# A hybrid GDN/HGRN2 block on one Trainium2 core: gates and HGRN values projected token-major, four heads at a time

## The chip, the cores and the metric

The kernel runs on one core of one Trainium2 chip. The metric is the device time of one execution in microseconds (us), as the median over runs. The engines are named as in the profile: PE (TensorE, matrix products into PSUM), DVE (VectorE), ACT (ScalarE), POOL (GpSimd) and SP (SyncE, which here only issues DMAs). Each engine works through its own instructions in order; semaphores hold an instruction until what it needs is done.

## The reference

One layer for 256 tokens (T) of width 2048 (D), all in float32:

```
n = rms_norm(h, norm_mix_w)
proj = n @ w_in                      # GDN: q, k, v, z and a, b;  HGRN2: q, f, i, g
# GDN, 8 heads of 128
qkv = silu(causal_conv4(qkv));  q, k l2-normalized
o = gated_delta_rule_chunked(q, k, v, beta, g)       # chunks of 64, a unit-lower system per chunk
y_a = head_rms_norm(o, norm_w) * silu(z)
# HGRN2, 8 heads of 128
forget = lb + (1 - lb) * sigmoid(f);  key = (1 - lb) * sigmoid(-f)
o = hgrn2_chunked(silu(q), key, i, log(forget))
y_b = head_rms_norm(o, norm_w) * silu(g)
h = h + concat(y_a, y_b) @ w_out
h = h + relu(rms_norm(h, norm_ffn_w) @ w1)**2 @ w2
out = rms_norm(h, norm_final_w)
```

In head_rms_norm the mean of squares runs over the 128 columns of a head, one value for each token and head.

## The kernel before

**Weights.** Every weight matrix streams through as tiles of 128 x 2048 (1 MB), 208 in all: 64 for the input projection (w_in), 16 for w_out, 64 each for the two feed-forward products (FF1, FF2). SP loads them in order into three buffers (`wpool`). To keep float32 accuracy, `split` (L111) cuts each half of a tile (1024 columns) into `hi`, rounded by ACT to fp32r (L117), and `lo`, the rest, by DVE (L118); the pairs lie in three buffers (`spool`). The activations are split once in the same way (`xT`, `hT`, `yTa`, `yTb`: first T columns hi, next T lo). PE computes hi·hi, hi·lo and lo·hi.

**Input projection.** `project` (L265) is feature-major: it takes two tiles and forms two 128-feature outputs over all 256 tokens. The weight is the stationary operand; one product of 512 columns (L281: both parts of `xT`) and one of 256 (L282) form a pair, 16 pairs for each tile. Two accumulators from `psA` (four PSUM banks of 512 columns in all) hold the result. L288 to L290 sum the two halves (ACT and DVE) and scale by `rB`, the norm's reciprocal for each token as a row repeated on every partition (DVE for HGRN, POOL for GDN). A head calls `project` twice: GDN for q, k and then v, z; HGRN for q, f and then i, g.

**Mixer.** Eight GDN heads (`gdn_mix`), each: convolution (L320, L322), silu, the gate SZ from z (L329), transposed v, normalized q and k, the key products `pk` and `pk`'s second half (L363, L364), whose decayed results (L367) are stored to DRAM (`scr_a`, L373). After the eighth, `gdn_invert` (L406) inverts all 32 x 32 diagonal blocks on POOL in 31 steps between L413 and the DMA of L424, and loads them back as `Xn` (L427). Eight HGRN heads follow (`hgrn_mix`): sigmoids, gate SZ (L531), scan (L542), ten operations on 256 columns for the decays of five levels (L548 and L563, five each), small products into `pd` and `pa` (L578 to L593), masks (L596, L600), the matrix `A`, and the head's output `poh`, 128 features by 256 tokens (L612, L613). `gdn_solve` (L430) finishes the triangular solve from the first HGRN head on (`SOLVE_AT` 9) and forms the GDN outputs two heads at a time. `finish_heads` squares the output, sums over features with a product by a matrix of ones (`pm`, L393 and L394, also hi and lo), takes the reciprocal root over all tokens and features (L395, L396), multiplies by it and by SZ (L397, L398) and splits the result into `yTa` (heads 0 to 11) or `yTb` (12 to 15).

**Order.** The body names heads in sequence, each head's projection one ahead of its mix; a tile framework with a scheduler then interleaves the instructions of each engine, and the order is fixed when the program is built. Buffers that are declared once (`bufs=1`) make a later writer wait for the last reader.

**Rest.** w_out runs as two halves of the output columns, eight tiles each, over the 16 heads' `yT`; the last product of the first half needs head 15's `yTb`. FF1 and FF2 follow. `h` (2 MB, the residual) is loaded by SP before the last two w_in tiles, into the memory that holds PA (key matrices of the first five heads).

Of the kernel before, what the change touches and what calls it, by code (L numbers as in the profile page):

```python
# [73 lines left out]
def hybrid_block(ctx: ExitStack, tc: tile.TileContext, x, xt, w_in, w_ab, params, w_out, w_ff1, w_ff2,  # L74
# [80 lines left out]
    sums = mp.tile([P, 4, T], F32, tag="u", name="sums")  # L155
# [109 lines left out]
    def project(base, hd, chunk, dsts):  # L265
        accs = [acc_a() for _ in range(2)]
        for kh in range(2):
            first = base == 0 and hd == 0 and chunk == 0
            if first:
                w = w_first[kh]  # L270
            else:
                w = wtile()
                SP.dma_start(w, w_in[((base > 0) * NH + hd) * 4 + chunk * 2 + kh])
# [12 lines left out]
        for g in range(2):  # L286
            lot = mp.tile([P, T], F32, tag="lot", name="lot", bufs=2)
            ACT.copy(lot, accs[g][:, T:])  # L288
            DVE.tensor_tensor(out=lot, in0=accs[g][:, 0:T], in1=lot, op=ALU.add)
            (POOL if base == 0 else DVE).tensor_tensor(out=dsts[g], in0=lot, in1=rB, op=ALU.mult)  # L290
# [15 lines left out]
    def gdn_project(hd):  # L306
        pre = mp.tile([P, 4, T], F32, tag="gx", name="pre").rearrange("p a t -> p (a t)")[:, 0:3 * (T + 3)]
        pre = pre.rearrange("p (a t) -> p a t", a=3)
        R = mp.tile([P, 4, T], F32, tag="R", name="R", bufs=RB)
        POOL.memset(pre[:, :, 0:3], 0.0)  # L310
# [4 lines left out]
    def gdn_mix(hd, pre, R):
        for i in range(3):
# [9 lines left out]
        DVE.scalar_tensor_tensor(out=u, in0=R, scalar=0.0, in1=u, op0=ALU.min, op1=ALU.subtract)
# [20 lines left out]
        DVE.tensor_tensor(out=qk, in0=qk, in1=u[:, 2:4, :], op=ALU.mult)  # L347
# [33 lines left out]
    def finish_heads(h0, nh, po, sz, scale, bank):  # L381

        n = nh * T
# [5 lines left out]
        shi = mp.tile([P, n], F32R, tag="Xn" if nh == 2 else "sh", name="shi")  # L389
        slo = mp.tile([P, n], F32R, tag="Yd" if nh == 2 else "vv", name="slo")  # L390
        ACT.copy(shi, sq)
        DVE.tensor_tensor(out=slo, in0=sq, in1=shi.bitcast(F32), op=ALU.subtract)
        PE.matmul(pm, lhsT=ones_r, rhs=shi, start=True, stop=False)  # L393
        PE.matmul(pm, lhsT=ones_r, rhs=slo, start=False, stop=True)  # L394
        ACT.activation(sq, pm, AF.Ln, bias=eps, scale=scale / P)  # L395
# [3 lines left out]
        src, hs = (yTa, h0) if h0 < NYA else (yTb[0], h0 - NYA)  # L399
        yv = sq.rearrange("p (a t) -> p a t", a=nh)  # L400
        hi, lo = src[:, hs:hs + nh, 0:T], src[:, hs:hs + nh, T:]
        split(yv, None, hi, lo)
# [27 lines left out]
    def gdn_solve(Xn):  # L430
# [67 lines left out]
        for pair in range(NH // 2):  # L498
            po = sv("po")
            for n in range(2):  # L500
                hd, c = 2 * pair + n, n * T
                PE.matmul(po[:, c:c + T], lhsT=V[:, hd, 0, :], rhs=PA(hd)[:, 0, 0:T], start=True, stop=False)
                PE.matmul(po[:, c + P:c + T], lhsT=V[:, hd, 1, :], rhs=PA(hd)[:, 0, T:384], start=False, stop=True)
            finish_heads(2 * pair, 2, po, SZ[:, 2 * pair:2 * pair + 2, :].rearrange("p a t -> p (a t)"), 1.0 / P, sv)


    def hgrn_project(hd):
        R = mp.tile([P, 4, T], F32, tag="R", name="R", bufs=RB)
        project(4112, hd, 0, (R[:, 0, :], R[:, 1, :]))
        project(4112, hd, 1, (R[:, 3, :], R[:, 2, :]))  # L510
        return R

    def hgrn_mix(hd, R):

        pv = mx("pvh")
        for hf in range(2):
            PE.transpose(pv[:, hf * P:(hf + 1) * P], R[:, 3, hf * P:(hf + 1) * P], ident)
        vv = mp.tile([P, 2, P], F32, tag="vv", name="vv")
        ACT.copy(vv.rearrange("p a e -> p (a e)"), pv[:, 0:T])
        u = mp.tile([P, 4, T], F32, tag="u", name="u", bufs=UB)  # L520
        sigmoid_parts(u[:, 0:3, :], R[:, 0:3, :], 3 * T)
        DVE.scalar_tensor_tensor(out=u[:, 3, :], in0=R[:, 1, :], scalar=0.0, in1=u[:, 1, :], op0=ALU.max, op1=ALU.add)
        DVE.scalar_tensor_tensor(out=u[:, 0:3, :], in0=R[:, 0:3, :], scalar=0.0, in1=u[:, 0:3, :],
                                 op0=ALU.min, op1=ALU.subtract)
# [6 lines left out]
        DVE.scalar_tensor_tensor(out=SZ[:, (NH + hd) % NRING, :], in0=R[:, 2, :], scalar=gnw[:, 1:2], in1=u[:, 2, :],  # L531
                                 op0=ALU.mult, op1=ALU.mult)
# [294 lines left out]
```

## Time and profile before

| what | before |
|---|---|
| median of 3 runs | 1277.36 us (1276.52 to 1277.49) |
| the profiled execution | 1277.5 us, span 1275.6 us |
| mean granted PE clock in it | 0.99 |
| last head's `poh` (L612), start | 496.38 us |
| FF1, first product (L704) | 555.44 us |
| weights and others moved | 229.65 MB, mean 180 GB/s |

The span runs from the first to the last instruction that the trace shows. Times in quoted rows count from its start. A timeline row holds: start, duration, engine, line, operation, output<-inputs, shapes, count, and in brackets how long the engine stood idle before it and what ended that. A group row holds: line, engine, operation, names, shapes, count | busy us, mean ns of one | idle us before them and what ended most of it. A windows row holds for one stretch the busy time of each engine with its number of instructions, then the granted PE clock (1.00 is full), the share of DMA time and GB/s.

### The profile page before, as it was taken

How to read it: one execution, taken by the hardware profiler on the slowest of the kernel's cores; microseconds unless marked ns; L12 is line 12 of the kernel's file. 1: busy time of each engine (PE TensorE's matmuls, PEld its weight loads, DVE VectorE, ACT ScalarE, POOL GpSimd, SP SyncE). 2: the span in 40 equal slices, each digit the busy share in tenths (PEclk: the TensorE clock that was granted, in tenths of full speed). 3: DMA queues.
4: the chain of work that ended last, by engine and by line, in shares of the span. 5: the costliest groups of instructions: out<-in, count | busy, mean ns of one | idle time of the engine just before them, and what ended most of it. 6: DMA issues, size and time to landing. Idle time of an engine off the chain costs nothing.

```text
span 1275.6 us, 18490 instructions
## 1 busy us (share of the span) xinstructions
PE 1243.4 (97%) x7290; PEld 1054.2 (83%) x7290; DVE 857.5 (67%) x1200; ACT 674.2 (53%) x972; POOL 178.7 (14%) x224
## 2 busy tenths in 40 slices
PE   6999999998999999999999999999999999999997
PEld 5888888877788887888888888888888888888885
DVE  8789999889978996566555565555555555555556
ACT  7567677655667774555444444444444444444453
POOL 4233433278310130000000000000000000000000
PEclk9999999998999998999999999999999999999999
DMA  7445555543424544455555555555555555555552
GB/s 290 167 154 192 172 177 190 182 141 131 151 101 169 196 165 165 160 203 198 177 187 197 173 191 191 176 195 185 178 198 199 197 195 189 188 191 195 198 203 95
DMA packets 34646, 229.65 MB, mean 180 GB/s; under 512 B 4408, under 2 KB 5184, under 8 KB 7808
## 3 DMA queue, kind: packets, MB, share of 16 engines
q1 hardware_dynamic: 32256, 225.32, 50.1%
q0 software_dynamic: 1728, 2.11, 1.3%
q8 instruction: 57, 0.93, 0.3%
q10 hardware_dynamic: 576, 1.05, 0.2%
q14 instruction: 29, 0.24, 0.1%
HBM read 225.83 MB, written 2.63 MB: 179 GB/s over the span
## 4 chain that ended last, share of the span: by engine, by line
PE 91%; DVE 3%; POOL 3%; issue 2%; DMA 1%; ACT 0%; SPq 0%; POOLq 0%; DVEq 0%; ACTq 0%
PE acc L281 15%; PE acc L721 14%; PE accb L721 13%; PE accb L704 9%; PE acc L704 9%; PE acc L282 8%; PE acc L659 7%; PE accb L705 5%; PE acc L705 5%; POOL Xt L419 1%; POOL X L421 1%; DVE xT L163 1%; DMA big<-in_xt_dram 1%; PE pk L363 1%; DVE E L548 0%
## 5 line engine op out<-in xcount | busy, mean ns | idle before, releaser
L118 DVE TENSOR_TENSOR lo<-w,hi 128x1024 fp32r<-128x1024 f32 x408 | 511.9, 1256 | 362.9 <-ACT hi L117 362.3
L117 ACT CAST hi<-w 128x1024 fp32r<-128x1024 f32 (+1 forms) x416 | 432.7, 1042 | 442.4 <-PE accb L721 177.0
L281 PE MATMUL acc<-xT,hi 128*128 128x512 f32 x1024 | 363.7, 401 | 10.0 <-ACT hi L117 8.3
L282 PE MATMUL acc<-xT,lo 128*128 128x256 f32 x1024 | 283.6, 286 | 4.5 <-DVE lo L118 4.3
L281 PEld LDWEIGHTS acc<-xT,hi 128*128 128x128 f32 x1024 | 192.1, 191 | 50.1 <-ACT hi L117 8.3
L282 PEld LDWEIGHTS acc<-xT,lo 128*128 128x128 f32 x1024 | 195.7, 192 | 11.6 <-DVE lo L118 5.8
L704 PE MATMUL acc<-hT,hi 128*128 128x512 f32 x512 | 181.3, 399 | 0.0
L704 PE MATMUL accb<-hT,hi 128*128 128x512 f32 x512 | 180.8, 398 | 0.0
L721 PE MATMUL accb<-hi,gs 128*128 128x512 f32 x496 | 170.5, 389 | 0.0
L705 PE MATMUL accb<-hT,lo 128*128 128x256 f32 x512 | 143.2, 281 | 0.0
L705 PE MATMUL acc<-hT,lo 128*128 128x256 f32 x512 | 142.8, 281 | 0.0
L721 PE MATMUL acc<-hi,gs 128*128 128x512 f32 x496 | 133.4, 389 | 0.0
L704 PEld LDWEIGHTS accb<-hT,hi 128*128 128x128 f32 x512 | 96.1, 188 | 23.8
L704 PEld LDWEIGHTS acc<-hT,hi 128*128 128x128 f32 x512 | 96.1, 188 | 23.3
L159 POOL TENSOR_TENSOR fin<-fin,cst 128x1 f32<-128x1 f32 x2 | 1.1, 566 | 776.9 <-PE accb L721 769.5
L721 PEld LDWEIGHTS accb<-hi,gs 128*128 128x128 f32 x496 | 93.1, 188 | 19.4
L721 PEld LDWEIGHTS acc<-hi,gs 128*128 128x128 f32 x496 | 93.1, 188 | 19.2
L705 PEld LDWEIGHTS acc<-hT,lo 128*128 128x128 f32 x512 | 96.5, 189 | 0.2
L705 PEld LDWEIGHTS accb<-hT,lo 128*128 128x128 f32 x512 | 96.5, 189 | 0.1
L721 PE MATMUL accb<-lo,gs 128*128 128x512 f32 x248 | 95.8, 389 | 0.0
L721 PE MATMUL acc<-lo,gs 128*128 128x512 f32 x248 | 77.2, 389 | 0.0
L721 PEld LDWEIGHTS accb<-lo,gs 128*128 128x128 f32 x248 | 46.6, 188 | 9.7
(248 smaller groups left out, 1275.2 us busy)
## 6 DMA issues: line engine op xcount, KB each, us to landing
w<-in_w_ff_dram SPq DMA_DIRECT2D x128, 1024.0 KB, 4.9
w<-in_w_in_dram SPq DMA_DIRECT2D x62, 1024.0 KB, 5.0
w<-in_w_out_dram SPq DMA_DIRECT2D x16, 1024.0 KB, 4.9
big<-in_xt_dram SPq DMA_DIRECT2D x4, 512.0 KB, 7.7
w<-in_w_in_dram SPq DMA_DIRECT2D x4, 512.0 KB, 7.9
h<-in_x_dram SPq DMA_DIRECT2D x2, 1024.0 KB, 9.0
dt<-scr_g POOLq DMA_DIRECT2D x8, 128.0 KB, 5.6
nfw<-in_norm_final_w_dram SPq DMA_DIRECT2D x1, 1024.0 KB, 4.4
```

The source lines that it names most:

```text
L117: ACT.copy(hi, w)
L118: eng.tensor_tensor(out=lo, in0=w, in1=hi.bitcast(F32), op=ALU.subtract)
L163: DVE.scalar_tensor_tensor(out=dst[:, k, T:2 * T], in0=pt, scalar=wcol, in1=dst[:, k, 0:T].bitcast(F32), op0=ALU.mult, op1=ALU.subtract)
L281: PE.matmul(accs[g], lhsT=hi[:, kk, g, :], rhs=xT[:, k, :], start=(k == 0), stop=False)
L282: PE.matmul(accs[g][:, T:], lhsT=lo[:, kk, g, :], rhs=xT[:, k, 0:T], start=False, stop=(k == KT - 1))
L363: PE.matmul(pk0, lhsT=R[:, 1, 0:P], rhs=qk.rearrange("p a t -> p (a t)"), start=True, stop=True)
L419: POOL.tensor_tensor(out=t3, in0=X[:, j, j + 1:].unsqueeze(2).to_broadcast([np_, nr, ncol]), in1=X[:, j, 0:ncol].unsqueeze(1).to_broadcast ...
L421: POOL.tensor_tensor(out=X[:, j + 1:, 0:ncol], in0=X[:, j + 1:, 0:ncol], in1=t3, op=ALU.subtract)
L659: PE.matmul(accs[2 * hf + c], lhsT=st, rhs=ww[:, c * 512:(c + 1) * 512], start=(k == 0 and a == 0 and ww is hi), stop=(k == 2 * NH - 1 and ...
L704: PE.matmul(accs[f], lhsT=hi[:, cs], rhs=hT[:, k, :], start=(k == 0), stop=False)
L705: PE.matmul(accs[f][:, T:], lhsT=lo[:, cs], rhs=hT[:, k, 0:T], start=False, stop=(k == KT - 1))
L721: PE.matmul(accs[hf][c], lhsT=gs[:, a + hf * P:a + hf * P + P], rhs=ww[:, cs], start=(f == 0 and a == 0 and ww is hi), stop=(f == NF - 1 a ...
```

## The change

What was feature-major for each head becomes token-major for four heads at once, for three of the eight outputs: the HGRN values i, the HGRN gates g and the GDN gates z.

- `project_tokens` takes four tiles and forms 512 features (four heads) for both token halves: `xT` is now the stationary operand and the weight the moving one, 24 products of 512 columns for each tile (L318). The two accumulators are copied out by ACT alone, with the norm's factor as a per-partition scale (`rcol`, L322). Results go to single tiles `vi`, `szg`, `szz`, which the second group of four heads reuses. 24 of the 64 tiles go this way.
- `gates_tokens` applies silu to such a group once, on 1024 columns (L325 onwards); the gates SZ of each head, with the norm weight in them, are gone.
- `project` now serves q and k (or q and f) of a head, and v of two GDN heads. The sigmoid work of a GDN head has 768 columns in place of 1024, that of an HGRN head 512 in place of 768.
- Mixer outputs are token-major: `po` and `poh` have tokens on the partitions, so i needs no transpose.
- `finish_heads` squares on ACT with a row sum for each head and token half (L439), takes the reciprocal root of those sums only (L440, L441), and scales each 128 x 128 block by it and by the gate in one DVE operation (L445). PE then transposes the result (`pt`, L452), and ACT and DVE split it with the norm weight as scale (L458, L459).
- The order of heads in the body is new. After the inversion: g's first group, q/f of head 1, mix 0, z's first group, q/f 2, solve, finish of GDN heads 0 to 3, mix 1, z's second group, q/f 3, finish of GDN heads 4 to 7, mix 2, q/f 4, mix 3, i's second group, g's second group, and then q/f and mixes of heads 4 to 7. (i's first group and q/f 0 are projected during the last GDN head.)

The core of the diff:

```
-        project(0, hd, 0, (pre[:, 0, 3:], pre[:, 1, 3:]))
-        project(0, hd, 1, (pre[:, 2, 3:], R[:, 3, :]))
...
+    def project_tokens(tag, name):
+        accs = [acc_a() for _ in range(2)]
+        for kq in range(4):
+            w, _ = w_next()
+            for q in range(2):
+                hi, lo = split(w[:, q * 1024:(q + 1) * 1024], 1024)
+                for kk in range(2):
...
+                    for hf in range(2):
+                        for a, ww in ((0, hi), (T, hi), (0, lo)):
+                            PE.matmul(accs[hf], lhsT=xT[:, k, a + hf * P:a + hf * P + P], rhs=ww[:, cs],
+                                      start=(k == 0 and a == 0 and ww is hi), stop=(k == KT - 1 and ww is lo))
+        dst = mp.tile([P, 2, 512], F32, tag=tag, name=name)
+        for hf in range(2):
+            ACT.activation(dst[:, hf, :], accs[hf], AF.Copy, scale=rcol[:, hf:hf + 1])
+        return dst
+
+    def gates_tokens(tag, name):
+        Z = project_tokens(tag, name)
+        u = mp.tile([P, 2, 512], F32, tag="gx", name="uz", bufs=2)
+        sigmoid_parts(u, Z, 1024)
+        DVE.scalar_tensor_tensor(out=u, in0=Z, scalar=0.0, in1=u, op0=ALU.min, op1=ALU.subtract)
+        ACT.activation(u, u, AF.Exp)
+        DVE.tensor_tensor(out=Z, in0=Z, in1=u, op=ALU.mult)
+        return Z
...
-        sq = mp.tile([P, n], F32, tag=f"fsq{nh}", name="fsq", bufs=1)
-        ACT.activation(sq, po, AF.Square)
-        pm = bank("pm")[:, 0:n]
...
-        ACT.activation(sq, pm, AF.Ln, bias=eps, scale=scale / P)
-        ACT.activation(sq, sq, AF.Exp, scale=-0.5)
-        DVE.tensor_tensor(out=sq, in0=po, in1=sq, op=ALU.mult)
-        DVE.tensor_tensor(out=sq, in0=sq, in1=sz, op=ALU.mult)
...
-        split(yv, None, hi, lo)
+        for hf in range(2):
+            for n in range(nh):
+                ACT.activation(sq, po[hf][:, n * P:(n + 1) * P], AF.Square, accum_out=ss[:, hf, n:n + 1])
+        ACT.activation(ss, ss, AF.Ln, bias=eps, scale=scale / P)
+        ACT.activation(ss, ss, AF.Exp, scale=-0.5)
...
+                DVE.scalar_tensor_tensor(out=y[:, hf, s], in0=po[hf][:, s], scalar=ss[:, hf, n:n + 1], in1=sz[:, hf, s],
+                                         op0=ALU.mult, op1=ALU.mult)
...
+            pt = bank("pt")[:, 0:w * T]
...
+                    PE.transpose(pt[:, n * T + hf * P:n * T + hf * P + P], y[:, hf, (m * w + n) * P:(m * w + n + 1) * P],
+                                 ident)
...
+            ACT.activation(hi, pt, AF.Copy, scale=gnw[:, group:group + 1])
+            DVE.scalar_tensor_tensor(out=lo, in0=pt, scalar=gnw[:, group:group + 1], in1=hi.bitcast(F32), op0=ALU.mult,
+                                     op1=ALU.subtract)
...
+    hgrn_mix(0, qf[0], vi, sz)
+    szz = gates_tokens("szz", "szz")
+    qf.append(hgrn_qf())
+    gdn_solve(Xn)
+    gdn_finish(0, szz)
+    hgrn_mix(1, qf[1], vi, sz)
+    szz = gates_tokens("szz", "szz")
+    qf.append(hgrn_qf())
+    gdn_finish(1, szz)
+    hgrn_mix(2, qf[2], vi, sz)
+    qf.append(hgrn_qf())
+    hgrn_mix(3, qf[3], vi, sz)
+    vi = project_tokens("vi", "vi")
+    sz = gates_tokens("szg", "szg")
+    for n in range(4, NH):
+        if n + 1 < NH:
+            qf.append(hgrn_qf())
+        hgrn_mix(n, qf[n], vi, sz)
```

The order that the scheduler makes of this is shown at three places. The first is PE around head 3's output. Before, `poh` of that head stands between projection products (L281, L282 are the pair of `project`; `pw_3088` belongs to the solve):

```order
L281 MATMUL acc<-xT,hi 128x512
L282 MATMUL acc<-xT,lo 128x256
L281 MATMUL acc<-xT,hi 128x512
L485 MATMUL pw_3088<-V,Y 128x128 x4
L282 MATMUL acc<-xT,lo 128x256
L281 MATMUL acc<-xT,hi 128x512
L612 MATMUL poh<-A,vv 128x256
L613 MATMUL poh<-A,vv 128x128
L282 MATMUL acc<-xT,lo 128x256
```

Now, on PE at the same place, from head 2's transposes on (L295 and L296 are the pair of `project`, here for head 5's q and f; L318 would be a token-major projection):

```order
L452 MATMUL pt<-cst,szg 128x128 x2
L631 MATMUL pd<-E 32x32 x32
L634 MATMUL pd<-gx 32x64 x8
L640 MATMUL pa<-E 32x32 x4
L644 MATMUL pa<-E 64x64 x2
L646 MATMUL pa<-L 128x128
L665 MATMUL poh<-vi,A 128x128
L666 MATMUL poh<-vi,A 128x128
L667 MATMUL poh<-vi,A 128x128
L295 MATMUL acc<-xT,hi 128x512
L296 MATMUL acc<-xT,lo 128x256
```

The projection products that stood among a head's small products have moved: none stands between head 2's transposes and head 3's output, and the next projection comes behind both.

The second place is ACT at the same heads (`A` is a head's matrix, L439 reads its output, L322 copies a token-major group out of its accumulators), as it is now:

```order
L663 COPY A<-pa 32x2x32 x2
L439 ACTIVATE fsq,ss<-poh 128x128
L322 ACTIVATE vi<-acc,rcol 128x512 x2
L439 ACTIVATE fsq,ss<-poh 128x128
L440 ACTIVATE ss<-ss,cst 128x2
L441 ACTIVATE ss<-ss 128x2
L458 ACTIVATE yTa<-pt,gnw 128x256
L322 ACTIVATE szg<-acc,rcol 128x512 x2
L117 CAST hi<-w 128x1024
```

The copies of i's second group (`vi`) stand behind the first reading of head 3's output, and those of g's second group (`szg`) behind that head's finish. Before, no such copy exists: two of L288 follow each projection.

The third place is SP's list of loads:

```order
-L273 DMA w<-in_w_in_dram 128x2048 x60
-L642 DMA h<-in_x_dram 128x2048 x2
-L273 DMA w<-in_w_in_dram 128x2048 x2
...
+L280 DMA w<-in_w_in_dram 128x2048 x56
+L715 DMA h<-in_x_dram 128x2048 x2
+L280 DMA w<-in_w_in_dram 128x2048 x6
```

The residual's two loads stand ahead of the last six w_in tiles now, in place of the last two. POOL's list loses the HGRN operations of heads that now come after the inversion in the order; its 31 steps are the same.

More of the change, by code (lines that the diff above doesn't have):

```diff
@@ L154, in hybrid_block @@
     junk = mp.tile([P, 1024], F32, tag="big", name="junk")
-    sums = mp.tile([P, 4, T], F32, tag="u", name="sums")
+    sums = mp.tile([P, 4, T], F32, tag="gx", name="sums", bufs=2)
+    rcol = cpool.tile([P, 2], F32, tag="rcol", name="rcol")
     def rstd(dst, src):
@@ L176, in row_scales @@
             PE.matmul(prb[:, 0:T], lhsT=ones, rhs=sums[:, c, :], start=(c == 0), stop=(c == 3))
+        for hf in range(2):
+            for c in range(4):
+                PE.matmul(prb[:, T + hf:T + hf + 1], lhsT=sums[:, c, hf * P:(hf + 1) * P], rhs=ones[:, 0:1],
+                          start=(c == 0), stop=(c == 3))
         ACT.activation(rB, prb[:, 0:T], AF.Ln, bias=eps, scale=1.0 / D)
         ACT.activation(rB, rB, AF.Exp, scale=-0.5)
+        ACT.activation(rcol, prb[:, T:T + 2], AF.Ln, bias=eps, scale=1.0 / D)
+        ACT.activation(rcol, rcol, AF.Exp, scale=-0.5)
     par = cpool.tile([P, 6, NH], F32, tag="par", name="par")
@@ L262, in gates, with w_next, project @@
         POOL.dma_start(scr_g, gr)
-    def project(base, hd, chunk, dsts):
+    tiles = [0]
+    def w_next():
+        n = tiles[0]
+        tiles[0] += 1
+        if n < 2:
+            return w_first[n], True
+        w = wtile()
+        SP.dma_start(w, w_in[n])
+        return w, False
+    def project(dsts, eng=POOL):
         accs = [acc_a() for _ in range(2)]
         for kh in range(2):
[L268 to L273, printed above, removed]
+            w, first = w_next()
             for q in range(2):
@@ L304, in hybrid_block, with pre, gdn_qk, gdn_v @@
     scr_x = dpool.tile([NH, 2, 4, 32, 32], F32, tag="scr_x", name="scr_x")
[L306 to L310, printed above, removed]
-        project(0, hd, 0, (pre[:, 0, 3:], pre[:, 1, 3:]))
-        project(0, hd, 1, (pre[:, 2, 3:], R[:, 3, :]))
-        return pre, R
-    def gdn_mix(hd, pre, R):
+    pres = {}
+    def pre(hd):
+        if hd not in pres:
+            p = mp.tile([P, 4, T], F32, tag="gx", name="pre", bufs=2).rearrange("p a t -> p (a t)")[:, 0:3 * (T + 3)]
+            pres[hd] = p.rearrange("p (a t) -> p a t", a=3)
+            POOL.memset(pres[hd][:, :, 0:3], 0.0)
+        return pres[hd]
+    def gdn_qk(hd):
+        p = pre(hd)
+        project((p[:, 0, 3:], p[:, 1, 3:]))
+    def gdn_v(pair):
+        project([pre(2 * pair + n)[:, 2, 3:] for n in range(2)])
+    def gdn_mix(hd):
+        pre = pres[hd]
+        R = mp.tile([P, 3, T], F32, tag="R", name="R", bufs=RB)
         for i in range(3):
@@ L379, in yT, with finish_heads @@
         return yTa[:, k, a:b] if k < NYA else yTb[0][:, k - NYA, a:b]
[L381 to L383 removed]
+    def finish_heads(h0, nh, po, sz, group, scale, bank):
         if h0 >= NYA and not yTb:
             yTb[0] = ypool.tile([P, 2 * NH - NYA, 2 * T], F32R, tag="yb", name="yTb")
[L386 to L402 removed]
@@ L497, in gdn_solve @@
             ACT.copy(V[:, hs, 1, :], pw.rearrange("p (a e) -> p a e", a=4))
[L498 to L504, printed above, removed]
@@ L507, in hgrn_project, with gdn_finish @@
[L507 to L510, printed above, removed]
-        return R
[L513 to L523, printed above, removed]
+    def gdn_finish(quad, sz):
+        po = [sv("po") for _ in range(2)]
+        for n in range(4):
+            hd, s = 4 * quad + n, slice(n * P, (n + 1) * P)
+            PE.matmul(po[0][:, s], lhsT=PA(hd)[:, 0, 0:P], rhs=V[:, hd, 0, :], start=True, stop=True)
+            PE.matmul(po[1][:, s], lhsT=PA(hd)[:, 0, P:T], rhs=V[:, hd, 0, :], start=True, stop=False)
+            PE.matmul(po[1][:, s], lhsT=PA(hd)[:, 0, T:384], rhs=V[:, hd, 1, :], start=False, stop=True)
+        finish_heads(4 * quad, 4, po, sz, 0, 1.0 / P, mx)
@@ L531, in hgrn_mix @@
[L531 to L532 removed]
+        DVE.tensor_scalar(KQ[:, 0, :], u[:, 2, :], oml[:, hd:hd + 1], None, ALU.mult)
         lf = view(u, 0, [[2 * T, 2], [1, T]])
```

100 lines of the change are left out of this document (66 added, 34 removed).

## The prediction

> **What bounds the kernel now.** I read the page first (busy shares, then the chain that ended last), then windows of the stretch that the change rewrites, then TensorE's idle rows in it.
>
> ```profile
> PE 1243.4 (97%) x7290; PEld 1054.2 (83%) x7290; DVE 857.5 (67%) x1200; ACT 674.2 (53%) x972; POOL 178.7 (14%) x224
> ...
> PE 91%; DVE 3%; POOL 3%; issue 2%; DMA 1%; ACT 0%; SPq 0%; POOLq 0%; DVEq 0%; ACTq 0%
> PE acc L281 15%; PE acc L721 14%; PE accb L721 13%; PE accb L704 9%; PE acc L704 9%; PE acc L282 8%; PE acc L659 7%; PE accb L705 5%; PE acc L705 5%; POOL Xt L419 1%; POOL X L421 1%; DVE xT L163 1%; DMA big<-in_xt_dram 1%; PE pk L363 1%; DVE E L548 0%
> ```
>
> Over the whole program TensorE (PE) is the bound: 1243.4 of a span of 1275.6 us. The stages differ, though. The windows give start:end, length, then busy time of PE, weight loads, VectorE (DVE), ScalarE (ACT), GpSimd (POOL), and the granted clock:
>
> ```profile
> core 0: us, PE busy (x) PEld busy (x) DVE busy (x) ACT busy (x) POOL busy (x), PEclk, DMA share, GB/s
> 33.00:247.00 214.00, 214.00 (x1200) 182.20 (x1199) 188.01 (x264) 145.72 (x206) 71.17 (x82) 1.00 0.54 177
> 247.00:335.00 88.00, 78.21 (x611) 66.20 (x613) 76.91 (x121) 48.30 (x82) 65.55 (x91) 0.92 0.41 141
> 335.00:504.00 169.00, 166.06 (x1576) 142.37 (x1561) 142.94 (x258) 115.38 (x200) 25.45 (x32) 1.00 0.45 158
> 504.00:556.00 52.00, 51.73 (x225) 42.47 (x226) 27.07 (x32) 23.21 (x31) 0.00 (x0) 0.94 0.47 164
> ```
>
> In the GDN stage (33 to 247) PE never stops, but DVE is already at 188.01 of 214. In 247 to 335 (the inversion on POOL beside the first HGRN heads) PE loses 9.79 us and runs at 0.92. These are its idle rows, with the last wait of the mixer at 504:
>
> ```profile
> 289.13 0.58 PE L282 MATMUL acc<-xT,lo 128*128 128x256 f32 x1 [2.81 <-DVE lo L118]
> ...
> 297.99 0.33 PE L578 MATMUL pd<-E 128*32 128x32 f32 x16 [1.08 <-DVE E L563]
> ...
> 302.53 0.79 PE L593 MATMUL pa<-L 128*128 128x128 f32 x2 [1.63 <-DVE L L567]
> ...
> 324.45 0.33 PE L517 MATMUL pvh<-cst,R 128*128 128x128 f32 x1 [1.19 <-ACT fsq L395]
> 326.13 0.80 PE L282 MATMUL acc<-xT,lo 128*128 128x256 f32 x2 [1.35 <-DVE lo L118]
> ...
> 504.27 2.93 PE L659 MATMUL acc<-hi,yTb 128*128 128x512 f32 x6 [2.93 <-ACT yTb L117]
> ```
>
> DVE ends most of them. So the mixer is a race between PE and DVE, and the order in which each in-order engine meets its work decides who waits.
>
> **The change, by stretches.** I lay the changed order along these markers of before, and sum where the last head's `yTb` lands (504.25); w_out's second half, FF1 and FF2 are untouched behind it.
>
> ```profile
> 245.90 0.59 PE L364 MATMUL pk<-R 128*128 128x256 f32 x2
> ...
> 247.85 1.08 POOL L373 DMA_DIRECT2D scr_a<-PA  x2 [17.08 <-DVE PA L367]
> ...
> 259.59 1.38 POOL L413 TENSOR_SCALAR_AFFINE_SELECT X<-X 64x1024 f32<-64x1024 f32 x1 [2.52 <-DMA X<-scr_a]
> ...
> 325.41 0.62 POOL L424 DMA_DIRECT2D scr_x<-X  x1
> ...
> 334.58 0.24 PE L453 MATMUL pP<-Xn,big 32*32 32x32 f32 x2
> ...
> 504.25 0.43 DVE L118 TENSOR_TENSOR yTb<-fsq,yTb 128x256 fp32r<-128x256 f32 x1 [0.47 <-ACT yTb L117]
> ...
> 555.44 0.48 PE L704 MATMUL acc<-hT,hi 128*128 128x512 f32 x1
> ```
>
> PE's prices come from steady spacings: eight feature-major pairs (512 plus 256 columns) between the first two rows below, seven 512-column products between the last two.
>
> ```profile
> 249.92 0.39 PE L281 MATMUL acc<-xT,hi 128*128 128x512 f32 x1
> ...
> 252.70 0.39 PE L281 MATMUL acc<-xT,hi 128*128 128x512 f32 x1
> ...
> 1250.26 1.75 PE L721 MATMUL acc<-keep,gs 128*128 128x512 f32 x7
> 1251.85 0.62 PE L721 MATMUL acc<-hi,gs 128*128 128x512 f32 x2
> ```
>
> A pair takes 2.78/8 = 0.3475 us, so a feature-major tile (16 pairs) 5.56; a 512-column product takes 1.59/7 = 0.227, so a token-major tile (24 of them) 5.45. A 256-column one is the difference, 0.12, which I take for a 128-column transpose too, as an upper end. 24 tiles at 0.11 less are −2.7; the norm sums (8 of 512 and 16 of 256 columns) go, −3.7; 16 more transposes cost +1.9; eight tiny products for `rcol` under +1. PE's own work falls by about 4 us: no gain by itself worth much. DVE's rows:
>
> ```profile
> L118 DVE TENSOR_TENSOR lo<-w,hi 128x1024 fp32r<-128x1024 f32 x141 | 185.1, 1314 | 33.3 <-ACT hi L117 32.7
> ...
> L289 DVE TENSOR_TENSOR lot<-acc,lot 128x256 f32<-128x256 f32 x64 | 26.4, 414 | 1.7 <-ACT lot L288 1.6
> L548 DVE TENSOR_TENSOR E<-gx 128x256 f32<-128x256 f32 x40 | 18.4, 520 | 2.2 <-POOL gx L543 2.2
> L290 DVE TENSOR_TENSOR R<-lot,rB 128x256 f32<-128x256 f32 x32 | 16.6, 519 | 0.2
> L563 DVE TENSOR_TENSOR E<-E,gx 128x256 f32<-128x256 f32 x40 | 16.2, 464 | 0.0
> L326 DVE SCALAR_TENSOR_TENSOR u<-R,u 128x1024 f32<-128x1024 f32 x8 | 9.8, 1225 | 4.5 <-issue 4.5
> L347 DVE TENSOR_TENSOR R<-R,u 128x512 f32<-128x512 f32 x8 | 8.7, 1094 | 0.0
> ...
> L564 DVE TENSOR_TENSOR E<-E,gx 128x512 f32<-128x512 f32 x8 | 5.4, 678 | 0.0
> ...
> L567 DVE TENSOR_TENSOR L<-E,ec 128x256 f32<-128x256 f32 x8 | 3.3, 410 | 0.0
> ...
> L355 DVE TENSOR_TENSOR dt<-dt,nsc 128x128 f32<-128x128 f32 x8 | 2.2, 280 | 0.0
> ```
>
> 24 sums (L289, −9.9) and 16 scalings (L290, −8.3) go with the feature-major g, z and i; the gates and the finishes become cheaper too. DVE loses near 30 us up to the last head. So the change relieves the engine that PE waits for. What it moves decides whether that is cashed.
>
> **A, start to the last GDN head's key products (246.4 before).** By the order PE has 37.2 feature-major tiles ahead of them before, and 27.4 plus 8 token-major ones now: 206.9 against 195.8 us, −11; with `rcol`, −10. But DVE, at 88% before, keeps its GDN work and its halves of the weight tiles in a stage 10 us shorter: about level with PE. Nothing in before shows a DVE-bound GDN stage. Its slack there, 26 us, excludes a wait far above 9 (once 10 are gone and the waits come in bursts of 1 to 3 us as in the gaps); bounds 0 to 9, and I take +4, the middle, since no row is nearer to one end. So 240.
>
> **B, to the first product of the solve.** The inversion runs on POOL from 247.85 to 325.41 and the solve starts at 334.58: 86.7 us. In before three HGRN heads put their own POOL operations into the inversion (the 65.8 us from L413 to L424 hold them); now one or two heads do. I take 81 plus 1.5 from the key products to the DMA, nearer to 86.7 than to the lower end of 74, since the 31 steps themselves stay; PE's own work to there is 68. So 322.5. PE has run out of what it may do some 7 us earlier; this wait replaces the five gaps above.
>
> **C, the solve to head 1's `pd`.** PE's own work here, counted in the order, is 14.4 us of feature-major and 21.8 of token-major products (i's second group is projected inside the solve), with the solve's, output and transposing products 51. The solve is a chain of small products and copies that fillers can't cover entirely; 55 to 64, I take 60, nearer to 51 plus a few hops of a microsecond or two, as the gaps of 1 to 3 us above. So 382.5.
>
> **D, head 1's `pd` to head 3's `poh`.** Here the change puts a new wait. PE's queue after the last g product holds `pt`, head 2's `pd` to `poh`, head 3's `pd` to `poh`, and only then q/f products. There are four accumulator banks: two hold i's second group, which ACT may not copy out until head 3's product has read the first group from the single `vi`; two hold g's second group, which waits for `szg`. So no projection can cover heads 2 and 3. DVE's work in the stretch, from the order: eight weight halves at 1.231 (tail row below), 9.8; two heads at 5 × 0.520 + 5 × 0.464 + 6.7 for a dozen smaller operations (L564, L567 show the sizes) = 11.6 each; 14 scaled 128-column operations at L355's 0.280 (an estimate; 0.464 is the upper end), 3.9; transposed parts 2.6; z's gate (L326 and L347) 2.3; head 1's mask 1.1 and two scalings 1.0: 44 us. PE has 29 there. I take 46, with two microseconds for the last chain to `poh`; ends 38 (some done early in C, where DVE idles) and 51. So 428.5.
>
> **E, to the last head's `yTb`.** The tail of before:
>
> ```profile
> 453.00:474.50 21.50, 21.50 (x185) 17.50 (x184) 20.72 (x40) 16.34 (x28) 3.34 (x7) 1.00 0.46 155
> 474.50:496.40 21.90, 21.90 (x187) 18.02 (x186) 16.18 (x27) 12.27 (x21) 3.04 (x4) 1.00 0.51 186
> ...
> L118 DVE TENSOR_TENSOR lo<-w,hi 128x1024 fp32r<-128x1024 f32 x15 | 18.5, 1231 | 4.8 <-ACT hi L117 4.7
> ...
> h<-in_x_dram SPq DMA_DIRECT2D x2, 1024.0 KB, 9.0
> ```
>
> Left are six q/f tiles, four heads, and w_out's first half. DVE: 27 halves, 33.2; four heads, 43; sums and scalings of six accumulators, 5.6; finishes 4.3; g's gate 2.3: 88.6 us. PE has 84. In the two tail windows DVE was busy 36.90 of 43.40 us, 85%. Ends 88.6 and 104; I take 95, as DVE is now the bound and idles less, with the clock's return after D inside it. So 523.5 against 504.25: **+19**, all behind it unchanged.
>
> ACT gains more small operations but is busy 115 of 169 us in the third window, so I cost them at nothing; without that cover they would lengthen each finish by a microsecond. On SP the two `h` loads pass ahead of the last six tiles: 9.0 us of landing, hidden as PE stands in D; uncovered, up to 9.
>
> **The sum** is against the profiled execution, 1277.5 us, 0.14 above the median of 1277.36: 1277.5 + 19.2 = 1296.7, say **1297**.
>
> **A rule against the row.** The page shows what one stop costs:
>
> ```profile
> 288.00:292.00 4.00, 2.87 (x9) 2.49 (x10) 4.00 (x6) 1.26 (x2) 3.88 (x5) 0.54 0.46 127
> ```
>
> After the gap of 2.81 us the granted clock is 0.54. The Trainium skill, page "TensorE: Matmul & The Clock Gate", section "A second HAM failure mode: psum-queue depth-cycling", says that frequent short idles between groups of products while accumulator banks are cycled make the clock switch between half and full. No run here shows repeated switching; by that rule the third rival below holds.
>
> **Rivals.**
> *R1, the relief decides.* If the scheduler's order leaves DVE ahead, so that heads 2 and 3 are nearly done when g's products end, the losses of before vanish: 9.8 idle and 7.0 of clock (0.08 × 88) in the second window, 2.9 and 3.1 (0.06 × 52) in the last, 22.8 together; half of D's excess (17/2) stays. 1277.5 − 22.8 + 8 = 1263. For it: DVE falls by 30 us. Against: four banks, one `vi`, heads 2 and 3 in a row. Chance 0.16.
> *R2, a wash.* C and E run at their lower ends and D at 38: 5 + 6 + 8 less: 1278. Chance 0.08.
> *R3, slower still: the clock.* It decides if PE, paced by DVE in A, C and D, stops for over 1 to 3 us at least four times more than before: the second window's 7.0 us of clock stand behind two longer stops (2.81 and 1.63), so 3.5 each, 14 in all: 1311. For it: the 0.54 above. Against: half rate where PE waits anyway is free. Chance 0.14.
> *That i, g and z don't move* can be ruled out by the order.
>
> **Numbers.** Forecast (1297, with its own range 1284 to 1308) 0.62. The range of eight in ten runs from 1272 to 1315: it takes in the wash and nearly all of R3, and leaves R1 out. Faster by over 0.2% (2.6 us, about what a measurement tells from none): R1 and a part of the wash, 0.20. Same: 0.06. Slower: 0.74.
>
> **What would show it.** Right: a PE gap of 10 to 20 us ahead of the first q/f product after head 3's `poh`, released by ACT's copy of `vi`, with a low clock behind it; the solve's first product waiting for POOL's `Xn`; DVE at 95% or more in A. Wrong: no such gap, or a last `yTb` earlier than 504. The step that I trust least is D, since a part of heads 2 and 3 may be done while DVE has slack in C.

## The result and the profile after

The changed kernel takes 1306.58 us (median of 4 runs, 1305.94 to 1308.61), against 1277.42 for the kernel before beside it: a ratio of 1.0231, 95% interval 1.0214 to 1.0249. It is slower by 29 us, where 19 were forecast. The profiled execution took 1305.94 us, with a span of 1304.1.

The page of the changed kernel, its busy shares and the chain that ended last:

```profile
PE 1250.4 (96%) x7138; PEld 1050.7 (81%) x7138; DVE 832.0 (64%) x1148; ACT 667.5 (51%) x1006; POOL 171.1 (13%) x216
...
PE 84%; DVE 6%; issue 3%; ACT 2%; POOL 2%; DMA 1%; SPq 0%; POOLq 0%; DVEq 0%; ACTq 0%
```

DVE is relieved as forecast (857.5 to 832.0 us, 25.5 less, where near 30 were forecast), yet the time rises. PE's share of the chain that ended last falls from 91% to 84%, and DVE's doubles. The markers of the prediction, in timeline rows of the changed kernel (the GDN key products' end, the first product of the solve, head 1's `pd`, head 3's `poh`, the last head's `yTb`, the start of FF1):

```profile
238.71 0.59 PE L413 MATMUL pk<-R 128*128 128x256 f32 x2
...
325.99 0.24 PE L511 MATMUL pP<-Xn,big 32*32 32x32 f32 x2
...
386.04 0.35 PE L631 MATMUL pd<-E 128*32 128x32 f32 x18
...
430.45 0.76 PE L665 MATMUL poh<-vi,A 128*128 128x128 f32 x2 [1.38 <-POOL A L656]
...
533.94 0.48 DVE L459 SCALAR_TENSOR_TENSOR yTb<-pt,gnw,yTb 128x256 fp32r<-128x256 f32 x1 [0.93 <-ACT yTb L458]
...
583.99 0.49 PE L777 MATMUL acc<-hT,hi 128*128 128x512 f32 x1
```

Up to the solve the changed kernel is ahead by 334.58 − 325.99 = 8.6 us. From there to the last `yTb` it takes 207.9 us in place of 169.7, a loss of 38.3; behind that it gains 1.1 (50.05 against 51.19). The sum, 28.5, is the difference of the two spans. So the whole loss lies between the solve and the last head. The windows over the same stretches, in the columns of the prediction's:

```profile
core 0: us, PE busy (x) PEld busy (x) DVE busy (x) ACT busy (x) POOL busy (x), PEclk, DMA share, GB/s
33.00:239.00 206.00, 205.17 (x1089) 171.74 (x1087) 168.01 (x241) 136.03 (x200) 60.09 (x73) 1.00 0.52 174
...
239.00:326.00 87.00, 75.45 (x426) 60.71 (x424) 69.88 (x90) 45.50 (x69) 64.30 (x86) 0.94 0.45 153
326.00:386.00 60.00, 57.13 (x508) 49.52 (x507) 29.74 (x42) 26.23 (x49) 0.00 (x0) 1.00 0.39 134
386.00:433.00 47.00, 35.57 (x409) 29.34 (x408) 37.69 (x77) 32.64 (x83) 10.25 (x14) 0.80 0.36 132
433.00:534.00 101.00, 92.75 (x783) 76.12 (x783) 78.22 (x145) 62.97 (x125) 20.66 (x23) 0.94 0.40 138
```

Read the DVE column downwards. Beside the solve (326 to 386) DVE is busy for half of the time, while PE works through token-major products. Directly behind it, from head 1's `pd` to the projection behind head 3's `poh`, it is PE that stands idle, 11.4 of 47 us, and its mean clock falls to 0.80. In the last stretch PE loses another 8.3 us and the clock is 0.94. Idle time of PE from the solve on is 22.6 us (before: 3.2). The low clock comes on top: 0.20 × 47 + 0.06 × 101 = 15 us if PE had been busy throughout, but much of it falls into the idle time. Counted over PE's busy time alone, in windows of 4 us from the solve to the start of FF1, it is an estimated 11.3 us (before: 2.8). So 19.4 us more of idle time and 8.5 more of low clock make up nearly all of the 28.5. How much of the low clock lies on the path that decides the time is not told by this sum. PE's idle rows there:

```profile
414.25 0.95 PE L631 MATMUL pd<-E 128*32 128x32 f32 x64 [2.63 <-DVE yTa L459]
...
421.48 0.76 PE L665 MATMUL poh<-vi,A 128*128 128x128 f32 x2 [4.17 <-issue]
...
425.41 0.66 PE L452 MATMUL pt<-cst,szg 128*128 128x128 f32 x2 [2.31 <-DVE szg L445]
...
433.15 0.80 PE L295 MATMUL acc<-xT,hi 128*128 128x512 f32 x1 [1.08 <-ACT vi L322]
...
522.56 0.66 PE L452 MATMUL pt<-cst,szg 128*128 128x128 f32 x2 [4.48 <-DVE szg L445]
...
532.90 0.49 PE L452 MATMUL pt<-cst,szg 128*128 128x128 f32 x2 [1.95 <-DVE szg L445]
```

The first four, with the 1.38 us ahead of head 3's `poh` above, are heads 2 and 3 with nothing beside them; the next projection waits for ACT's copy of `vi`, as the order said. The last two are the transposes of the last two heads, which wait for DVE's scaled outputs while the products of w_out's first half around them are no cover.

### The profile page after: what moved, and what is told of

Same layout as the page of the kernel before. It is cut to its first block, busy times and chain, and to the rows that moved or that the text cites. A ratio compares the mean times of both kernels' runs of the same rounds, so it can differ in the third digit from the quotient of the medians.

```text
span 1304.1 us, 18162 instructions
## 1 busy us (share of the span) xinstructions
PE 1250.4 (96%) x7138; PEld 1050.7 (81%) x7138; DVE 832.0 (64%) x1148; ACT 667.5 (51%) x1006; POOL 171.1 (13%) x216
## 3 DMA queue, kind: packets, MB, share of 16 engines
HBM read 225.83 MB, written 2.63 MB: 175 GB/s over the span
## 4 chain that ended last, share of the span: by engine, by line
PE 84%; DVE 6%; issue 3%; ACT 2%; POOL 2%; DMA 1%; SPq 0%; POOLq 0%; DVEq 0%; ACTq 0%
PE acc L794 13%; PE accb L794 13%; PE accb L777 9%; PE acc L777 9%; PE acc L295 8%; PE acc L318 8%; PE acc L732 6%; PE acc L778 5%; PE accb L778 5%; PE acc L296 4%; DVE lo L118 1%; DVE E L601 1%; ACT hi L117 1%; DVE E L616 1%; DMA big<-in_xt_dram 1%
## 5 line engine op out<-in xcount | busy, mean ns | idle before, releaser
L295 PE MATMUL acc<-xT,hi 128*128 128x512 f32 x640 | 229.8, 406 | 11.3 <-ACT hi L117 8.3
L296 PE MATMUL acc<-xT,lo 128*128 128x256 f32 x640 | 176.4, 287 | 0.8 <-DVE lo L118 0.6
L295 PEld LDWEIGHTS acc<-xT,hi 128*128 128x128 f32 x640 | 120.2, 192 | 37.2 <-ACT hi L117 8.3
L296 PEld LDWEIGHTS acc<-xT,lo 128*128 128x128 f32 x640 | 122.8, 192 | 6.0 <-DVE lo L118 1.1
L318 PE MATMUL acc<-hi,xT 128*128 128x512 f32 x384 | 117.7, 401 | 0.0
L794 PEld LDWEIGHTS accb<-hi,gs 128*128 128x128 f32 x496 | 93.1, 188 | 19.4
L318 PEld LDWEIGHTS acc<-hi,xT 128*128 128x128 f32 x384 | 73.3, 193 | 15.3
```

The lines of the kernel that those rows point to most:

```text
L295: PE.matmul(accs[g], lhsT=hi[:, kk, g, :], rhs=xT[:, k, :], start=(k == 0), stop=False)
L296: PE.matmul(accs[g][:, T:], lhsT=lo[:, kk, g, :], rhs=xT[:, k, 0:T], start=False, stop=(k == KT - 1))
L318: PE.matmul(accs[hf], lhsT=xT[:, k, a + hf * P:a + hf * P + P], rhs=ww[:, cs], start=(k == 0 and a == 0 and ww is hi), stop=(k == KT - 1 a ...
L794: PE.matmul(accs[hf][c], lhsT=gs[:, a + hf * P:a + hf * P + P], rhs=ww[:, cs], start=(f == 0 and a == 0 and ww is hi), stop=(f == NF - 1 a ...
```

## The experiments

Three theories were set against each other at first. **Banks**: the four held accumulator banks make the gap. **DVE floor**: DVE idles beside the solve and has more work behind it than the rest of the mixer has time. **Finish chain**: the new finish is too long. Ratios are against the kernel before, measured beside each run. It took 1277.42 us beside the change and 1276.1 to 1276.4 beside the experiments, so a difference of two medians below holds about 1 us that is not the edit's: by the ratios e1_both gains 8.6 us over the change and e5_spread 23.9, where the medians say 10.6 and 25.7.

**e1_both** frees the banks.

```
-    vi = project_tokens("vi", "vi")
-    sz = gates_tokens("szg", "szg")
+    vi = project_tokens("PA1", "vi")
+    sz = gates_tokens("V", "szg")
```

> The second groups of i and g go into other memory (that of PA1 and V, free by then), so their accumulators need not wait for head 3. Banks theory (the four held accumulator banks cause the loss between head 1's small products and head 3's output: 11.9 us idle and 9.3 of clock): that gap goes, 1288 to 1294 us, the rest coming back at the tail. DVE-floor theory (DVE stands idle 29 us between the solve's start and head 1's pd, and has some 133 us of work behind it): the wait only moves to the tail, not below 386 + 133 = 519 for the last yTb against 533.9: 1296 to 1302. Finish-chain theory: no change beyond 3 us.

Measured: 1296.0 us, ratio 1.0164 (1.0143 to 1.0186), 10.6 less than the change. PE's idle rows of this run:

```profile
387.27 0.33 PE L452 MATMUL pt<-cst,szz 128*128 128x128 f32 x1 [2.68 <-DVE szz L445]
502.95 0.66 PE L452 MATMUL pt<-cst,szg 128*128 128x128 f32 x2 [4.72 <-DVE szg L445]
517.18 0.66 PE L452 MATMUL pt<-cst,szg 128*128 128x128 f32 x2 [5.77 <-DVE szg L445]
527.56 0.49 PE L452 MATMUL pt<-cst,szg 128*128 128x128 f32 x2 [1.95 <-DVE szg L445]
```

The gap at heads 2 and 3 is gone: between 387 and 503 no row with an idle time of half a microsecond is left. But the last heads now show 12.4 us of waits in place of 6.4 (the profiled execution, at 1300.6 us, was the longest of the four, so a part of this may be its own). The held banks made the gap; two thirds of the loss is elsewhere. The time lies at the lower end of what the DVE floor allowed, 1296 to 1302, and above the banks' 1288 to 1294.

**e2_mix1** and **e3_both** put head 1 ahead of the solve, alone and together with e1's edit.

```
+    hgrn_mix(1, qf[1], vi, sz)
     gdn_solve(Xn)
     gdn_finish(0, szz)
-    hgrn_mix(1, qf[1], vi, sz)
     szz = gates_tokens("szz", "szz")
```

> Only the order in the body changes: head 1's mix stands ahead of the solve and of the first GDN finish, buffers as in the change. DVE-floor theory: DVE works in the stretch where it stood idle, and all behind it comes earlier: 15 to 20 us less, 1287 to 1292. Banks theory: heads 2 and 3 still stand together between g's second group and the next projection, so PE's gap before that projection stays, and the time falls by less than 6: 1301 or more. Finish-chain theory: no change beyond 3 us.

> Both edits together. If the banks and the idle DVE are two losses, their gains add to some 28 us: 1275 to 1282. If they are two names of one loss, the time is that of the better of the two runs within 4 us.

Measured: 1310.14 (1.0264, 1.0248 to 1.0280) and 1296.87 us (1.0164, 1.0143 to 1.0184). Neither gains anything over the kernel with the same buffers. The window beside the solve in e3_both says why:

```profile
325.50:385.50 60.00, 57.27 (x498) 49.35 (x498) 28.62 (x37) 25.29 (x46) 0.00 (x0) 1.00 0.40 141
```

DVE is as idle there as before the edit (busy 28.62 of 60 us, against 29.74). Head 1's decays, most of its work on DVE, were already done ahead of the solve in the change (L616 from 293.28 on), so the edit moved little more than its small products, its mask and its finish; and head 2, still behind z's second group and the second GDN finish, did not move in. So this edit was no test of a busy DVE beside the solve; that had to wait for e5_spread.

**e4_nonorm** leaves the norm of the HGRN heads out.

```
+        if nh == 4:
             for hf in range(2):
                 for n in range(nh):
                     ACT.activation(sq, po[hf][:, n * P:(n + 1) * P], AF.Square, accum_out=ss[:, hf, n:n + 1])
...
-                DVE.scalar_tensor_tensor(..., scalar=ss[:, hf, n:n + 1], ...)
+                DVE.scalar_tensor_tensor(..., scalar=ss[:, hf, n:n + 1] if nh == 4 else 1.0, ...)
```

> The norm of the HGRN heads is left out (no squares with row sums, no reciprocal root on ACT; the scale is the constant 1), so each head's chain from poh to pt is some 1.2 to 1.5 us shorter. Finish-chain theory (the longer chain through ACT, DVE, PE, ACT, DVE is what costs): 8 heads at 1.2 or more, 10 us or more less, 1296 or below. The other two: only where no other work covers it (heads 2, 3 and the last two), 2 to 6 us less, 1301 to 1305.

Measured: 1296.48 us, 1.0166 (1.0149 to 1.0183): 10 us less by the medians and 8.3 by the ratios, about what the finish-chain theory said. That theory could not be dropped here, and e9 takes it up.

**e6_warm** fills PE's gaps with useless products.

```
+        if hd % 4 >= 2:
+            ps = sv("warm")
+            for i in range(4):
+                PE.matmul(ps, lhsT=ident, rhs=E[:, 0:2, :].rearrange("p a t -> p (a t)"), start=True, stop=True)
...
+            for i in range(3):
+                PE.matmul(ps[:, 0:384], lhsT=ident, rhs=A, start=True, stop=True)
```

> The change with useless products on PE, between the small products and the output, and behind the output, of heads 2, 3, 6 and 7 (4 of 512 columns and 3 of 384 for each, output never read). Clock theory: the gaps of 2 to 4 us stay filled, the granted clock stays above 0.9 through heads 2 and 3 and the two projections behind them, and the 15 us that the low clock costs from head 1 to the last head shrink by half or more: 6 to 10 us less, 1297 to 1301. If PE's low clock only fills time in which it waits for DVE anyway: within 3 us of 1306.6, or above, as the products lengthen the chain.

Measured: 1310.44 us, 1.0260 (1.0243 to 1.0277), 4 above the change. Two windows of the change, and of this run three windows around the same heads, with the fillers behind head 2's output and ahead of its transposes, and head 3's `poh`:

```profile
416.00:420.00 4.00, 1.31 (x6) 0.90 (x6) 3.33 (x8) 1.25 (x3) 1.77 (x3) 0.50 0.14 55
420.00:424.00 4.00, 1.62 (x6) 1.35 (x6) 2.97 (x8) 3.84 (x11) 0.15 (x1) 0.50 0.00 0
```

```profile
420.00:428.00 8.00, 3.52 (x69) 2.94 (x59) 6.33 (x16) 4.70 (x11) 1.91 (x3) 0.86 0.01 2
428.00:436.00 8.00, 7.84 (x110) 4.43 (x108) 3.45 (x9) 2.25 (x9) 0.10 (x1) 0.92 0.01 2
436.00:444.00 8.00, 6.37 (x34) 5.00 (x34) 0.82 (x3) 3.11 (x12) 0.76 (x2) 1.00 0.00 0
...
427.31 3.06 PE L675 MATMUL warm<-A,cst 128*128 128x384 f32 x6
...
430.21 3.60 PE L651 MATMUL warm<-E,cst 128*128 128x512 f32 x8
...
437.85 0.46 PE L669 MATMUL poh<-vi,A 128*128 128x128 f32 x2 [1.63 <-POOL A L660]
```

The granted clock rose from 0.50 to 0.86 and more, and the time rose too. But the fillers stood in the way of the heads' own products: between head 2's output and its transposes they hold PE for 6.3 us (427.31 to 433.65), and head 3's `poh` came at 437.85, 7.4 us later than in the change, while the solve began 1.3 later (327.3). So this run does not tell what the low clock cost: a gain from the clock and the fillers' own price are in one number. What a filler of no length would give back stays open.

**e5_spread** keeps every operation of the change and spreads them: heads and groups alternate, second groups go where memory is free, z's second group comes last, and w_out takes late what is finished late (the w_in tiles are loaded in the new order).

```
     szz = gates_tokens("szz", "szz")
     qf.append(hgrn_qf())
+    hgrn_mix(1, qf[1], vi, sz)
     gdn_solve(Xn)
+    qf.append(hgrn_qf())
+    hgrn_mix(2, qf[2], vi, sz)
     gdn_finish(0, szz)
-    hgrn_mix(1, qf[1], vi, sz)
-    szz = gates_tokens("szz", "szz")
-    qf.append(hgrn_qf())
-    gdn_finish(1, szz)
-    hgrn_mix(2, qf[2], vi, sz)
+    vj = project_tokens("X", "vi")
     qf.append(hgrn_qf())
     hgrn_mix(3, qf[3], vi, sz)
-    vi = project_tokens("vi", "vi")
-    sz = gates_tokens("szg", "szg")
-    for n in range(4, NH):
-        if n + 1 < NH:
-            qf.append(hgrn_qf())
-        hgrn_mix(n, qf[n], vi, sz)
+    sy = gates_tokens("szz", "szg")
+    qf.append(hgrn_qf())
+    hgrn_mix(4, qf[4], vj, sy)
+    qf.append(hgrn_qf())
+    hgrn_mix(5, qf[5], vj, sy)
+    szz = gates_tokens("szg", "szz")
+    qf.append(hgrn_qf())
+    hgrn_mix(6, qf[6], vj, sy)
+    gdn_finish(1, szz)
+    hgrn_mix(7, qf[7], vj, sy)
...
-        for kp in range(8):
+        korder = (0, 1, 4, 5, 6, 2, 3, 7)
+        for kp in korder:
```

> The same operations as in the change, in another order: i's and g's second groups go to other memory (the tags X and szz, free after the solve and the first GDN finish), the solve stands behind head 1, a head's mix stands behind each projection of two to four tiles, z's second group and the second GDN finish come last, and w_out takes those heads late. Packing theory (the loss is that PE-heavy groups and DVE-heavy heads stand in lumps, so DVE idles beside the solve and PE beside heads 2, 3 and the last two): 15 to 30 us less than the change, 1277 to 1292, with no PE gap over 3 us behind head 1. If instead the operations of the change themselves are too long for DVE and ACT: no less than the 1296 of the run with the banks freed.

Measured: 1280.83 us, 1.0044 (1.0024 to 1.0064): 25.7 of the 29 us are back. Its windows over the first three stretches of the mixer behind the GDN heads, and the longest idle row that PE has behind the solve:

```profile
239.00:326.00 87.00, 76.47 (x529) 61.68 (x527) 76.99 (x110) 49.73 (x87) 65.16 (x89) 0.92 0.39 134
326.00:386.00 60.00, 58.64 (x555) 50.33 (x556) 40.42 (x65) 32.27 (x56) 5.75 (x10) 0.97 0.42 145
386.00:433.00 47.00, 47.00 (x440) 40.48 (x439) 36.58 (x66) 32.85 (x70) 7.91 (x10) 1.00 0.53 185
...
494.47 0.73 PE L631 MATMUL pd<-E 128*32 128x32 f32 x62 [2.27 <-DVE yTa L459]
```

Beside the solve DVE works 40.42 us where it had 29.74, and from 386 to 433 PE is busy all of the time at full clock. The operations of the change are not too long; they stood badly. (The second groups of i and g have memory of their own here too, as in e1_both, so the order alone is not separated from that.)

**e5a_no_wout_order** is e5_spread with w_out's heads in sequence again; **e8_zlate** moves head 1 ahead of z's first group; **e9_spread_nonorm** is e5_spread without the norm of the HGRN heads, by e4's edit.

```
-        korder = (0, 1, 4, 5, 6, 2, 3, 7)         # e5a
-        for kp in korder:
+        for kp in range(8):
...
     hgrn_mix(0, qf[0], vi, sz)
+    qf.append(hgrn_qf())                          # e8
+    hgrn_mix(1, qf[1], vi, sz)
     szz = gates_tokens("szz", "szz")
     qf.append(hgrn_qf())
-    hgrn_mix(1, qf[1], vi, sz)
     gdn_solve(Xn)
-    qf.append(hgrn_qf())
```

> The spread order of e5_spread, but w_out takes the heads 0 to 15 in sequence as in the change, so its first half stops at GDN heads 4 to 7 until the second GDN finish, late in the mixer. If the cover of the last heads by w_out carries much of the 26 us that the spread order gained, PE stands still there: 8 to 20 us more than e5_spread, 1289 to 1301. If the spread of heads and groups ahead of it carries it: within 5 us, 1281 to 1286.

> As e5_spread, with q and f of head 2 and head 1's mix ahead of z's first group, and the solve behind q and f of head 3. Packing theory: before the solve DVE has 77 of 87 us and ends most of PE's gaps there; head 1's work comes earlier while z's products cover it, so some of the 10 us idle and 7 of clock go: 1272 to 1280. If POOL's inversion (242 to 329) sets that stretch whatever PE does: within 3 us of 1280.8.

> e5_spread with the norm of the HGRN heads left out, as in e4_nonorm. There it gave 10 us. If that was the chain of heads that nothing covered, little is left where projections cover it: 0 to 4 us less than e5_spread, 1277 to 1281. If the finish costs by its work on ACT and DVE wherever it stands: about 10 us again, 1269 to 1273.

Measured: e5a 1286.56 us (1.0077, 1.0061 to 1.0094), 5.7 more than e5_spread: w_out's order carries about a fifth of the gain, between the expectation's two cases ("within 5", 8 to 20). e8 1280.67 (1.0032, 1.0021 to 1.0043): no gain. In the window of e8_zlate before the solve

```profile
239.00:326.00 87.00, 76.25 (x556) 61.76 (x558) 75.39 (x110) 49.43 (x87) 66.80 (x91) 0.92 0.40 137
```

PE is as idle as in e5_spread. The first product of the solve says what ends this stretch, in e5_spread and then in e8_zlate:

```profile
326.86 0.24 PE L511 MATMUL pP<-Xn,big 32*32 32x32 f32 x2 [1.84 <-DMA Xn<-scr_x]
...
325.67 0.24 PE L511 MATMUL pP<-Xn,big 32*32 32x32 f32 x2 [0.32 <-DMA Xn<-scr_x]
```

PE waits there for the DMA that loads POOL's inverted blocks. So POOL's inversion and its DMAs set the stretch, as the second case of the expectation had it, and packing PE's work tighter ahead of it gained nothing. Whether DVE, for which POOL waits inside the inversion, makes it longer was not separated.

e9 1276.33 (1.0001, 0.9991 to 1.0010): the norm is worth 4.5 us where projections cover the heads, and was worth 10 in the change (by the ratios 5.5 and 8.3). So a third to a half of e4's gain was a chain that the order left uncovered, and the rest is what the norm costs in either order. The new finish is not the longer one, at least at the last head: from its `poh` to the end of its `yTb` the kernel before took 504.68 − 496.38 = 8.3 us, and the changed one 534.42 − 530.04 = 4.4, by this row of the changed kernel:

```profile
530.04 0.46 PE L665 MATMUL poh<-vi,A 128*128 128x128 f32 x2
```

No version that computes the reference beat the kernel before: the two best, e5_spread and e8_zlate, stand 0.3 to 0.4% above it.

## Why the prediction was nearly right, step by step

**The direction and the place** were right. The forecast mechanism, heads 2 and 3 uncovered between g's second group and the next projection, is in the trace, and e1_both removed it by the buffers alone. Of the three signs that the prediction named, one came in part: PE's gap is 11.6 us, with a low clock, but in five pieces (2.63, 4.17, 2.31, 1.38, 1.08), and only the last is released by ACT's copy of `vi`. The other two, the solve's first product waiting for `Xn` and DVE at 95% in A, did not come.

**C and D** landed on their numbers partly by luck. C was 60.0 us against 60, but the forecast had 51 of PE's own work and 9 of uncovered hops, and the window shows PE busy 57.13 and idle 2.9. D was 44.4 (386.04 to 430.45) against 46, but the forecast had 44 of DVE's work and 2 of a chain, and DVE was busy 37.69 in the window that runs on to 433: less work and more waits on chains between engines.

**A** landed at 239 against 240, by two errors that cancel. DVE, forecast level with PE and at 95% or more, was busy 168.01 of 206 us (20 less than before), and PE lost 0.83 there, not 4; the count of tiles promised 10 us less and the marker moved by 7.

**B** took 87 us against 82.5. The step said that the inversion sets it and that PE runs out of work some 7 us before its end. The first half holds, the second does not. PE had lost its time earlier, waiting for weight halves, and was still at q and f of head 2 when `Xn` came:

```profile
251.01 1.26 POOL L471 TENSOR_SCALAR_AFFINE_SELECT X<-X 64x1024 f32<-64x1024 f32 x1 [2.92 <-DMA X<-scr_a]
...
286.96 0.73 PE L318 MATMUL acc<-lo,xT 128*128 128x512 f32 x2 [2.49 <-DVE lo L118]
...
299.81 1.22 PE L318 MATMUL acc<-lo,xT 128*128 128x512 f32 x2 [3.98 <-DVE lo L118]
...
316.82 0.61 POOL L482 DMA_DIRECT2D scr_x<-X  x1 [0.30 <-POOL X L480]
320.13 2.64 POOL L485 DMA_DIRECT2D Xn<-scr_x  x4 [2.70 <-DMA scr_x<-X]
...
324.58 0.86 DVE L500 COPY XP<-Xn 32x512 f32<-32x512 f32 x2 [1.47 <-DMA Xn<-scr_x]
```

The four loads of `Xn` were issued from 320.13 to 322.1 and took 3.0 to 4.3 us to land; DVE's first reader waits for them, and the solve's first product at 325.99 follows at once. In e1_both PE itself waits there:

```profile
328.75 0.31 PE L511 MATMUL pP<-Xn,big 32*32 32x32 f32 x2 [3.00 <-DMA Xn<-scr_x]
```

What was mis-sized is the inversion. From its first operation to the DMA behind it, it takes 316.82 − 251.01 = 65.8 us, as before (325.41 − 259.59); the step had counted some 6 us less from the key products' DMA to the solve. POOL's rows in it say why: two HGRN heads still stand there, with 8.3 us of their own operations (before: 6.9), and POOL's waits for DVE went only from 6.3 to 3.8. The losses of before in this stretch (9.8 idle, clock 0.92) did not vanish, as the first rival had it: 11.5 idle, clock 0.94.

**E** was mis-sized most of all: 103.5 us (430.45 to 533.94) against 95, just inside the upper end of 104. The step said that DVE "is now the bound and idles less", with 88.6 us of DVE's work and 84 of PE's. (Its four heads stand in that sum at 43; at the 11.6 each of step D they are 46.) In the window from 433 to 534 it is the other way round: PE was busy 92.75 of 101 us, and DVE 78.22, 77%, less than the 85% of the tail before and ten less than the step's count. Three things show in the rows. The first is the clock. The next projection's first row is at 433.15, above; eight pairs later stands

```profile
438.43 0.40 PE L295 MATMUL acc<-xT,hi 128*128 128x512 f32 x1
```

These eight pairs took 5.28 us, where the prediction's price is 2.78. The second is in DVE's rows behind head 3:

```profile
434.54 0.61 DVE L445 SCALAR_TENSOR_TENSOR szg<-poh,ss,szg 128x128 f32<-128x128 f32 x2 [5.73 <-ACT ss L441]
440.65 0.48 DVE L459 SCALAR_TENSOR_TENSOR yTa<-pt,gnw,yTa 128x256 fp32r<-128x256 f32 x1 [5.50 <-ACT yTa L458]
```

The first wait is for ACT's norm of head 3, whose `poh` came at 430.45; the two copies of `vi` (1.26 us from 432.42) stand between ACT's two squares. In the second, DVE's next instruction needs ACT's, ACT's needs the transposes of head 3, and these stand on PE behind the first 11 pairs of the next projection (433.15 to 439.72), most of them slow. ACT and DVE have weight halves to split behind that wait and can't reach them. PE does not stop for this at once: from 434 to 522 its longest idle row is 0.65 us. The third is the last two heads, 4.5 and 2.0 us of PE's waits. That the 11 us which DVE lost behind head 3 are what makes the last heads late is likely, but no run separates it. None of the three is DVE's amount of work, which the step took for the bound.

**The rivals.** R1 needed heads 2 and 3 nearly done when g's products end; they weren't. The relief of DVE came but had nothing to shorten: PE's own work hardly changes, and where the order lets PE run (e5_spread) it gives the time of before within 0.4%. R3, the clock, is half right: the page "TensorE: Matmul & The Clock Gate" of the Trainium skill, section "A second HAM failure mode: psum-queue depth-cycling", has the clock switch under frequent short idles. The trace agrees so far that it stood at 0.50 from 416 to 424, among gaps of 1.1 to 4.2 us. The rival's own price, 14 us more than before, is not shown: the estimate above is 8.5 us more of low clock in PE's busy time, of which 2.5 are the eight slow pairs that DVE's second wait stands behind. e6_warm does not settle it, since its fillers cost PE time of their own.

What e1 to e9 leave open is the split of the 29 us into single causes: the banks (10.6) and the order of w_out (5.7) were measured with different rest, the clock was not separated, and the remainder belongs to the spread of heads as a whole.

## What to carry to other kernels

When work is grouped into larger pieces, count for each stretch what each engine has to do beside the others, not only the totals: a group that is heavy on one engine needs a partner that is heavy on another. A group's result in a single buffer holds its accumulators until the last reader of the group before, so look up which accumulators are free at the place where cover is needed. And a short finish still stops an in-order engine if its next step is queued on another engine behind a projection.

## What was not expected of the hardware

Short gaps were enough to slow what came behind them: after heads 2 and 3, where no single gap of PE is longer than 4.2 us, eight pairs of products took 5.28 us in place of 2.78. And a higher clock alone says nothing of the time: e6_warm filled the gaps, the granted clock went from 0.50 to between 0.86 and 1.00, and the kernel took 1310.44 us against 1306.58, since the fillers themselves stood in the heads' way.
